# Seven block products instead of eight in part of an output projection, and weight loads of 1 MB

## The chip, the cores and the metric

One NeuronCore of a Trainium2 chip runs the whole kernel. The metric is the device time of one execution in microseconds (us). The engines are named as in the profile: PE (TensorE matmuls; PEld is its weight load), DVE (VectorE), ACT (ScalarE), POOL (GpSimd) and SP, whose queue issues the DMAs.

## The reference

One decoder layer on 256 tokens of width 4096, in fp32. Cut to what matters:

```python
proj = x @ w_in                        # 256 x 4096 by 4096 x 11280
y_conv, y_gla, y_mem = ...             # three gated groups; mem @ w_mem_kv feeds the third
mixed = concatenate([y_conv, y_gla, y_mem], axis=-1)      # 256 x 4096
out = mixed @ w_out                                       # 4096 x 4096
y = layernorm(alpha * x + out) * ln_g + ln_b
```

## The kernel before

An fp32 value is kept as two parts that the PE multiplies exactly: ACT casts it to `hi`, DVE subtracts to get `lo` (`halves`, L88 to L90). A product of two such values takes three passes: hi by hi, lo of the activations by hi of the weights, hi by lo of the weights. The activations are the stationary operand (128 features by 128 tokens), 512 columns of weights the moving one, and the sum over the 32 k-tiles of 128 features stays in one of eight PSUM banks.

The program has three parts. First the memory projection (L148 to L180): for each k-tile two weight loads of 512 KB, for four banks each; every fourth k-tile also one 512 KB unit of `memT` and one of `xT`. Then 23 panels of `w_in`, and after them 8 panels of `w_out` (the loop `for n in range(8)` near the end). `panel` takes 16 chunks of two k-tiles: a 512 KB load into one of six `raw` buffers (`wraw`), `halves` into one of four `hi` and four `lo` buffers (`whi`, `wlo`, WBUFS = 4), 24 matmuls over two token tiles into two of the four `acc` banks. So a `lo` can be made only when PE is through with the `lo` four tiles earlier, and a load can start only when the tile six earlier has been split. The next panel has the other two banks; after a panel DVE adds its banks to the residual rows (`residual`, L929) and takes statistics, and POOL multiplies by the norm's gain.

Small work (transposes, norms, gates) stands in a list and is dealt out between the chunks by `do_work`. The temporaries `T` and `S` (4 KB a partition each) exist once. The order of the instructions on each engine and of the DMAs on SP is fixed when the program is built, by a scheduler that sees the dependences and its own estimates; each engine then works strictly in that order. All loads go through SP's one queue.

Of the kernel before, what the change touches and what calls it, by code (L numbers as in the profile page):

```python
# [25 lines left out]
WBUFS = 4  # L26
# [6 lines left out]
# (name, index, column ranges of w_in)  # L33
# [15 lines left out]
def layer_kernel(ctx, tc, xT, memT, xres, w_mem, w_in, w_out, cst, w_gate,  # L49
# [5 lines left out]
    wraw = ctx.enter_context(tc.tile_pool(name="wraw", bufs=6))  # L55
# [7 lines left out]
    # SBUF in units of 4 KB a partition, each handed out again once it is given back  # L63
# [78 lines left out]
    # the array's clock comes up while the first loads are under way  # L142
# [3 lines left out]
    for kt in range(KT):  # L146
        if kt == 0:
            mt0 = unit_tiles("mem")  # L148
            m_units.append(load(mt0, four(memT[0]), 0, 1))
        elif kt % 4 == 0:  # L150
            m_units.append(load(unit_tiles("mem"), four(memT[kt // 4])))
        mh, ml = m_units[kt // 4]
        for half in range(2):
            wt = w_tiles([P, 1024], "wm")
            step = 256 if kt == 0 and half == 0 else 512
            if kt == 0:
                for a in range(0, 1024, step):
# [79 lines left out]
    def queue_halves(src, then):  # L237
        """Token-major [P, 2, 512] -> feature-major hi and lo, for then(hi, lo)."""

        def scratch():  # L240
            serial[0] += 1
            return tmp.tile([P, 4, 256], F32, tag="S", name=f"S_{serial[0]}", bufs=1)

        def go(d):
# [298 lines left out]
    def queue_head(h):  # L543
# [273 lines left out]
    # y = (z g) rstd - mu rstd g + b: z g as z comes, the rest a product of -mu rstd and 1  # L817
    # with g and b, g hi in rows 0 and 32, lo in 64, b hi in row 1, lo in 65
# [115 lines left out]
    for n in range(8):  # L934
        if 2 <= n < 6:
            work.append(lambda n=n: rows_gb(n - 2))
# [3 lines left out]
        if n < 7:  # L940
            banks = panel(w_out[n], 512, stat, soon=KT // 2 if n else 10)
            g = spread(ln_g, n, "S")
            for tt in range(2):
                residual(tt, n, banks[tt])
                y = z[n][:, tt, :]
                nc.gpsimd.tensor_tensor(out=y, in0=y, in1=g, op=ALU.mult)

    # the last panel ends with the first token tile, so that its norm runs beside the second's
    banks, rest = panel(w_out[7], 512, stat, apart=APART)
# [38 lines left out]
def lay_out(inputs):  # L988
# [67 lines left out]
```

## Time and profile before

| | |
|---|---|
| three runs | 1541.33, 1542.21, 1542.31 us (median 1542.21) |
| profiled execution | span 1539.6 us, from its first to its last instruction; a run's time has some 2.6 us more around such a span |
| PE busy | 1526.9 us (99%) |
| DVE, ACT busy | 980.6 us (64%), 740.7 us (48%) |
| DMA | 307.56 MB, mean 200 GB/s |

PE busy is the share of time in which some matmul is under way; since matmuls overlap, the pace is read from the time that a stretch of them takes, not from the duration of one.

### The profile page before, as it was taken

The page shows a single profiled execution, that of the slowest core. Times are in us where ns is not written, and L with a number is a line of the kernel's source. Part 1 is how long each engine was busy: PE and PEld are TensorE (multiplying, and loading weights), DVE is VectorE, ACT ScalarE, POOL GpSimd, SP SyncE. Part 2 cuts the span into 40 slices and gives each one's busy share as a digit, 9 for nine tenths or more (in the row PEclk, how much of TensorE's full clock was granted, in tenths as well). Part 3 has the DMA queues.
Part 4 walks back from the last instruction along what each step waited for, and adds up shares of the span by engine and source line. Part 5 has one row for each costly group of instructions (what it writes and reads, how often), then busy time and mean ns, then how long its engine had stood idle before and what let it go on. Part 6 is the DMA issues. An engine that isn't in the chain of part 4 may idle for free.

```text
span 1539.6 us, 18667 instructions
## 1 busy us (share of the span) xinstructions
PE 1526.9 (99%) x6977; PEld 1292.9 (84%) x6977; DVE 980.6 (64%) x1227; ACT 740.7 (48%) x898; POOL 68.0 (4%) x71
## 2 busy tenths in 40 slices
PE   9999999999999999999999999999999999999997
PEld 7888888888888888999998888888888888888885
DVE  6555654999999555857575555555557555455555
ACT  6444653444566344655454554455556333333341
POOL 0000000000000000003030000000000000000001
PEclk9999999999999999999999999999999999999998
DMA  8777676666656666565555566666677666666662
GB/s 326 245 251 249 190 210 193 190 197 188 193 163 178 218 192 188 161 191 175 167 170 195 179 195 205 193 193 195 195 233 253 216 196 196 206 202 199 198 199 109
DMA packets 89363, 307.56 MB, mean 200 GB/s; under 512 B 9972, under 2 KB 10868, under 8 KB 89272
## 3 DMA queue, kind: packets, MB, share of 16 engines
q1 hardware_dynamic: 89272, 306.38, 63.0%
q8 instruction: 54, 0.88, 0.2%
q14 instruction: 37, 0.30, 0.1%
HBM read 302.14 MB, written 4.19 MB: 199 GB/s over the span
## 4 chain that ended last, share of the span: by engine, by line
PE 98%; DVE 1%; DMA 0%; issue 0%; SPq 0%; ACT 0%; POOL 0%; DVEq 0%; ACTq 0%
PE acc L279 85%; PE mk L169 5%; PE mv L169 5%; PE o L260 1%; PE A L561 1%; PE sc L260 0%; PE mo L260 0%; DMA rawwm<-w_mem 0%; DVE xr L915 0%; SPq L115 0%; PE mg L905 0%; DVE nz L502 0%; POOL xr L913 0%; DVE cc L870 0%; DVE low L90 0%
## 5 line engine op out<-in xcount | busy, mean ns | idle before, releaser
L90 DVE TENSOR_TENSOR low<-raww,hiw 128x1024 fp32r<-128x1024 f32 (+2 forms) x496 | 603.5, 1219 | 427.5 <-ACT hiw L89 422.3
L89 ACT CAST hiw<-raww 128x1024 fp32r<-128x1024 f32 (+2 forms) x496 | 507.6, 1027 | 640.7 <-PE acc L279 612.4
L279 PE MATMUL acc<-hiw,hx 128*128 128x512 f32 (+2 forms) x1472 | 560.3, 381 | 0.0
L279 PE MATMUL acc<-hiw,lx 128*128 128x512 f32 (+2 forms) x1472 | 560.3, 381 | 0.0
L279 PE MATMUL acc<-low,hx 128*128 128x512 f32 (+2 forms) x1472 | 381.6, 380 | 0.0
L279 PEld LDWEIGHTS acc<-hiw,hx 128*128 128x128 f32 x1472 | 276.4, 188 | 45.4
L279 PEld LDWEIGHTS acc<-hiw,lx 128*128 128x128 f32 x1472 | 276.3, 188 | 45.2
L279 PEld LDWEIGHTS acc<-low,hx 128*128 128x128 f32 x1472 | 275.3, 188 | 45.4
L279 PE MATMUL acc<-hiw,xh 128*128 128x512 f32 x512 | 199.3, 389 | 0.0
L279 PE MATMUL acc<-hiw,xl 128*128 128x512 f32 x512 | 199.2, 389 | 0.0
L279 PE MATMUL acc<-low,xh 128*128 128x512 f32 x512 | 137.8, 389 | 0.0
L279 PEld LDWEIGHTS acc<-hiw,xl 128*128 128x128 f32 x512 | 96.1, 188 | 20.0
L279 PEld LDWEIGHTS acc<-low,xh 128*128 128x128 f32 x512 | 96.1, 188 | 19.9
L279 PEld LDWEIGHTS acc<-hiw,xh 128*128 128x128 f32 x512 | 96.1, 188 | 19.9
L90 DVE TENSOR_TENSOR lowm<-rawwm,hiwm 128x1024 fp32r<-128x1024 f32 (+2 forms) x68 | 78.3, 1160 | 53.2 <-ACT hiwm L89 52.6
L649 DVE SCALAR_TENSOR_TENSOR cacc<-hT,cst_sb,cacc 128x231 f32<-128x231 f32 (+29 forms) x240 | 98.0, 462 | 0.1
L89 ACT CAST hiwm<-rawwm 128x1024 fp32r<-128x1024 f32 (+2 forms) x68 | 67.6, 1002 | 62.8 <-PE mv L169 30.9
L169 PE MATMUL mk<-hiwm,hmem 128*128 128x512 f32 (+1 forms) x132 | 50.7, 387 | 0.4 <-ACT hiwm L89 0.4
L169 PE MATMUL mk<-hiwm,lmem 128*128 128x512 f32 (+1 forms) x132 | 50.4, 384 | 0.0
L227 ACT COPY S<-T 32x256 f32<-32x256 f32 x112 | 45.2, 404 | 9.9 <-DVE T L212 8.5
L169 PE MATMUL mv<-hiwm,hmem 128*128 128x512 f32 x128 | 49.9, 390 | 0.0
L169 PE MATMUL mv<-hiwm,lmem 128*128 128x512 f32 x128 | 49.8, 389 | 0.0
(179 smaller groups left out, 752.5 us busy)
## 6 DMA issues: line engine op xcount, KB each, us to landing
raww<-w_in SPq DMA_DIRECT2D x288, 512.0 KB
raww<-w_out SPq DMA_DIRECT2D x128, 512.0 KB
rawwm<-w_mem SPq DMA_DIRECT2D x62, 512.0 KB
raww<-w_in SPq DMA_DIRECT2D x64, 412.0 KB
raww<-w_in SPq DMA_DIRECT2D x16, 416.0 KB
rawx<-xT SPq DMA_DIRECT2D x8, 512.0 KB
xr<-xres SPq DMA_DIRECT2D x8, 512.0 KB
out<-xr SPq DMA_DIRECT2D x16, 256.0 KB
```

Source lines behind the costliest of these rows:

```text
L89: nc.scalar.copy(out=hi, in_=src)
L90: nc.vector.tensor_tensor(out=lo, in0=src, in1=hi.bitcast(F32), op=ALU.subtract)
L169: nc.tensor.matmul(mem_banks[half * 4 + a // 512 * 2 + mt][:, a % 512 : a % 512 + step], lhsT=s[:, kt % 4, mt * P : (mt + 1) * P], rhs=w[: ...
L227: f(out=to[32 * b : 32 * b + 32, :, :, a, :], in_=frm[32 * a : 32 * a + 32, :, :, b, :],)
L260: nc.tensor.matmul(ps, lhsT=a, rhs=b, start=t == 0 and k == 0, stop=t == n - 1 and k == 2)
L279: nc.tensor.matmul(banks[tt][:, :width], lhsT=s[:, kt % 4, tt * P : (tt + 1) * P], rhs=w[:, k, :], start=kt == 0 and not second and s is s ...
L561: nc.tensor.matmul(ps[:, at : at + n], lhsT=keys[:, j, k0 : k0 + P], rhs=qs[:, j, q0 : q0 + n], start=dk == 0, stop=dk == 1,)
L649: nc.vector.scalar_tensor_tensor(out=a, in0=h, scalar=dw_sb[:, cb, j : j + 1], in1=a, op0=ALU.mult, op1=ALU.add)
```

## The change

Output panels 0 to 5 are taken in three pairs. A pair's chunk is 1 MB: two k-tiles by two panels, four blocks of weights, against two k-tiles by two token tiles of activations. A chunk taken "by eight" is two tiles of 12 matmuls (`b`, `a`). A chunk taken "by seven" (Winograd's form of Strassen's product) needs seven block products, 21 matmuls: tile `c` (3), then `a`, `y`, `x` (6 each). DVE makes `x` and `y` as differences of weight blocks first, in the single temporaries `T` (`tx`) and `S` (`ty`), and all four are split. The sums of activation blocks are made once for a unit (`sums`, also through `S` and `T`) and kept. By seven go 4 of the 16 chunks of the first pair and 6 of each other. A pair uses all eight banks, N, 4, 3, 2 of `acc` and 1, 5, 6, 7 of `sm`; at its end DVE combines them into the residual rows, by way of `U`, which is `T` again, and multiplies by the gain. Besides, all weights come in 1 MB loads into three `raw` buffers of 8 KB, and the units of `memT` and `xT` are loaded into buffers of the general pool instead of `raw` buffers. Panels 6 and 7 keep their form.

```diff
-    wraw = ctx.enter_context(tc.tile_pool(name="wraw", bufs=6))
+    wraw = ctx.enter_context(tc.tile_pool(name="wraw", bufs=3))
...
-            wraw.tile([P, 4, 256], F32, tag="raw", name=f"raw{name}_{serial[0]}"),
+            unit([P, 4, 256], F32, f"raw{name}"),
...
+    def load_unit(name, ap):
+        tiles = unit_tiles(name)
+        hi, lo = load(tiles, ap)
+        give(tiles[0])
+        return hi, lo
...
-            m_units.append(load(unit_tiles("mem"), four(memT[kt // 4])))
+            m_units.append(load_unit("mem", four(memT[kt // 4])))
+        raw = w_raw([P, 2, 1024], "wm")
+        if kt:
+            nc.sync.dma_start(out=raw, in_=w_mem[kt].rearrange("p (h n) -> p h n", h=2))
...
-            x_units.append(load(unit_tiles("x"), four(xT[kt // 4])))
+            x_units.append(load_unit("x", four(xT[kt // 4])))
...
-            tiles = w_tiles([P, 2, width], "w", KT // 2 - apart <= c < KT // 2 - WBUFS)
-            hi, lo = load(tiles, chunks[c].rearrange("p (k n) -> p k n", k=2))
+            if c % 2 == 0:
+                raw = w_raw([P, 4, width], "w")
+                nc.sync.dma_start(out=raw, in_=chunks[c // 2].rearrange("p (k n) -> p k n", k=4))
+            hi, lo = w_tiles([P, 2, width], "w", KT // 2 - apart <= c < KT // 2 - WBUFS)
+            halves(raw[:, 2 * (c % 2) : 2 * (c % 2) + 2, :], hi, lo)
...
+    def sums(hi, lo):
+        r = tmp.tile([P, 4, 256], F32, tag="S", name=f"r_{serial[0]}", bufs=1)
+        f = tmp.tile([P, 2, 4, P], F32, tag="T", name=f"f_{serial[0]}", bufs=1)
+        nc.vector.tensor_tensor(out=r, in0=hi.bitcast(F32), in1=lo.bitcast(F32), op=ALU.add)
+        r = r.rearrange("p (q k) (t c) -> p q k t c", q=2, t=2)
+        a11, a21, a12, a22 = (r[:, :, k, t, :] for k in range(2) for t in range(2))
+        s1, s2, s3, s4 = (f[:, :, j, :] for j in range(4))
+        for o, x, y, op in (
+            (s1, a21, a22, ALU.add),
+            (s2, s1, a11, ALU.subtract),
+            (s3, a21, a11, ALU.subtract),
+            (s4, a12, s2, ALU.subtract),
+        ):
+            nc.vector.tensor_tensor(out=o, in0=x, in1=y, op=op)
+        eh = unit([P, 2, 4, P], F32R, "eh")
+        el = unit([P, 2, 4, P], F32R, "el")
+        halves(f, eh, el)
+        return eh, el
+    def pair(chunks, order, stat, ext, soon=KT // 2):
+        banks = {}
+        for pool, tag, names in ((acc, "acc", "N432"), (sm, "sm", "1567")):
+            for nm in names:
+                banks[nm] = pool.tile([P, 512], F32, tag=tag, name=f"{tag}_{nm}_{serial[0]}")
+        def plain(k, tt):
+            return lambda c: tuple(
+                t[:, (2 * c + k) % 4, tt * P : (tt + 1) * P] for t in stat(c // 2)
+            )
+        def summed(j):
+            return lambda c: tuple(t[:, c % 2, j - 1, :] for t in ext(c // 2))
+        a11, a21, a12, a22 = (plain(k, tt) for k in range(2) for tt in range(2))
+        eight = (
+            ("b", ((1, a21, "N"), (0, a22, "N"), (1, a11, "3"), (0, a12, "3"))),
+            ("a", ((0, a21, "4"), (1, a22, "4"), (0, a11, "2"), (1, a12, "2"))),
+        )
+        seven = (
+            ("c", ((0, summed(4), "3"),)),
+            ("a", ((1, a12, "2"), (0, a11, "1"))),
+            ("y", ((1, a22, "4"), (0, summed(2), "6"))),
+            ("x", ((0, summed(1), "5"), (1, summed(3), "7"))),
+        )
...
+        for n, (c, by7, tiles) in enumerate(plan):
+            raw = w_raw([P, 4, 512], "w")
+            nc.sync.dma_start(out=raw, in_=chunks[c].rearrange("p (k n) -> p k n", k=4))
+            w = {}
+            if by7:
+                x = tmp.tile([P, 2, 512], F32, tag="T", name=f"tx_{serial[0]}", bufs=1)
+                y = tmp.tile([P, 2, 512], F32, tag="S", name=f"ty_{serial[0]}", bufs=1)
+                nc.vector.tensor_tensor(
+                    out=x,
+                    in0=raw[:, 3:4, :].to_broadcast([P, 2, 512]),
+                    in1=raw[:, 0:3:2, :],
+                    op=ALU.subtract,
+                )
+                nc.vector.tensor_tensor(
+                    out=y[:, 0, :], in0=raw[:, 2, :], in1=x[:, 0, :], op=ALU.subtract
+                )
+                nc.vector.tensor_tensor(
+                    out=y[:, 1, :], in0=raw[:, 1, :], in1=y[:, 0, :], op=ALU.subtract
+                )
+                src = dict(a=raw[:, 0:2, :], c=raw[:, 2:3, :], x=x, y=y)
+            else:
+                src = dict(a=raw[:, 0:2, :], b=raw[:, 2:4, :])
+            for nm, terms in tiles:
+                m = 1 if nm == "c" else 2
+                w[nm] = tuple(t[:, :m, :] for t in w_tiles([P, 2, 512], "w"))
+                halves(src[nm], *w[nm])
+                for second in range(2):
+                    for j, (slot, st, bk) in enumerate(terms):
+                        sh, sl = st(c)
+                        for s in (sh,) if second else (sh, sl):
+                            nc.tensor.matmul(
+                                banks[bk],
+                                lhsT=s,
+                                rhs=w[nm][second][:, slot, :],
+                                start=first[bk] == (n, nm, j) and not second and s is sh,
+                                stop=last[bk] == (n, nm, j) and second == 1,
+                            )
+            do_work(-(-len(work) // max(1, soon - n)))
+        return banks
...
-    for n in range(8):
-        if 2 <= n < 6:
-            work.append(lambda n=n: rows_gb(n - 2))
+    def load_res(n):
         xr = unit([P, 2, 512], F32, "xr")
         nc.sync.dma_start(out=xr, in_=xres[n].rearrange("p (t d) -> p t d", t=2))
         z.append(xr)
...
+    extT = {}
+    def make_sums(u):
+        extT[u] = sums(*stat(u))
+    def in_order(pattern, by7):
+        p7 = [c for c in range(KT // 2) if c // 2 in by7]
+        p8 = [c for c in range(KT // 2) if c // 2 not in by7]
+        return [(p7.pop(0), True) if ch == "7" else (p8.pop(0), False) for ch in pattern]
+    orders = (
+        in_order("8888888887878787", (4, 5)),
+        in_order("8878878878788787", (4, 5, 6)),
+        in_order("8878878878788787", (4, 5, 6)),
+    )
+    for u in (4, 5):
+        work.append(lambda u=u: make_sums(u))
+    for j in range(3):
+        if j == 1:
+            work.append(lambda: make_sums(6))
+        n0, n1 = 2 * j, 2 * j + 1
+        load_res(n0)
+        load_res(n1)
+        b = pair(w_pairs[j], orders[j], stat, lambda u: extT[u], soon=KT // 2 if j else 8)
+        rows = [spread(ln_g, n0, "Ah"), spread(ln_g, n1, "Al")]
+        def add(y, ps, first=False):
+            if first:
+                nc.vector.scalar_tensor_tensor(
+                    out=y, in0=y, scalar=ALPHA, in1=ps, op0=ALU.mult, op1=ALU.add
+                )
+            else:
+                nc.vector.tensor_tensor(out=y, in0=y, in1=ps, op=ALU.add)
+        z11, z21 = z[n0][:, 0, :], z[n0][:, 1, :]
+        z12, z22 = z[n1][:, 0, :], z[n1][:, 1, :]
+        add(z22, b["N"], True)
+        add(z12, b["3"], True)
+        add(z11, b["2"], True)
+        add(z21, b["4"], True)
+        t = tmp.tile([P, 2, 512], F32, tag="T", name=f"U_{serial[0]}", bufs=1)
+        u2, u3 = t[:, 0, :], t[:, 1, :]
+        nc.scalar.copy(out=u2, in_=b["1"])
+        add(z11, b["1"])
+        nc.vector.tensor_tensor(out=u2, in0=u2, in1=b["6"], op=ALU.add)
+        add(z12, b["5"])
+        add(z22, b["5"])
+        nc.vector.tensor_tensor(out=u3, in0=u2, in1=b["7"], op=ALU.add)
+        add(z12, u2)
+        add(z21, u3)
+        add(z22, u3)
+        for n, tt, y in ((n0, 0, z11), (n1, 0, z12), (n0, 1, z21), (n1, 1, z22)):
+            nc.vector.bn_stats(out=stats[:, tt, n, :], in_=y)
+            nc.vector.tensor_tensor(out=y, in0=y, in1=rows[n - n0], op=ALU.mult)
...
```

The first place is SP's queue in the memory projection. Before, from the first load of k-tile 3 (`rawwm_241`) to k-tile 4 (`rawwm_303`, `rawwm_321`):

```order
L115 DMA rawwm_241<-w_mem 128x1024
L984 DMA ng_sb<-norm_g 128x512
L115 DMA rawwm_259<-w_mem 128x1024
L115 DMA rawx_291<-xT 128x1024
L115 DMA rawmem_297<-memT 128x1024
L115 DMA rawwm_303<-w_mem 128x1024
L115 DMA rawwm_321<-w_mem 128x1024
L115 DMA rawwm_339<-w_mem 128x1024
```

After the change, from the load of k-tile 3 (`rawwm_236`) to that of k-tile 4 (`rawwm_296`); 128x2048 is 1 MB, the others 512 KB:

```order
L162 DMA rawwm_236<-w_mem 128x2048
L116 DMA rawmem_290<-memT 128x1024
L116 DMA rawx_432<-xT 128x1024
L116 DMA rawmem_438<-memT 128x1024
L116 DMA rawx_580<-xT 128x1024
L116 DMA rawmem_586<-memT 128x1024
L116 DMA rawx_728<-xT 128x1024
L116 DMA rawmem_734<-memT 128x1024
L116 DMA rawx_876<-xT 128x1024
L116 DMA rawmem_882<-memT 128x1024
L162 DMA rawwm_296<-w_mem 128x2048
```

Two unit loads stood between the two k-tiles' weights, and now nine stand there.

The second place is DVE behind an output panel. Before, the last three splits of panel 1 with the first of panel 2, the two `residual` additions and the statistics:

```order
L90 TENSOR_TENSOR low_9950<-raww_9948,hiw_9949 128x1024
L90 TENSOR_TENSOR low_9978<-raww_9976,hiw_9977 128x1024
L90 TENSOR_TENSOR low_9996<-raww_9994,hiw_9995 128x1024
L929 SCALAR_TENSOR_TENSOR xr_9644<-xr_9644,acc_9646 128x512
L929 SCALAR_TENSOR_TENSOR xr_9644<-xr_9644,acc_9647 128x512
L90 TENSOR_TENSOR low_10014<-raww_10012,hiw_10013 128x1024
L932 BN_STATS zstats<-xr_9644 128x6 x2
L90 TENSOR_TENSOR low_10032<-raww_10030,hiw_10031 128x1024
```

After the change, behind the first pair: the end of the combination (`xr` are residual rows, `row` the gain), the sums for unit 6 (`r`, `f`, `eh` and `el`), and the second pair's first chunk by seven, whose `tx` has the place of `f`, which had the place of `U`:

```order
L1114 BN_STATS zstats<-xr_8891 128x6
L347 TENSOR_TENSOR f_9604<-r_9603 128x2x128 x2
L1115 TENSOR_TENSOR xr_8891<-xr_8891,row_9533 128x512
L1115 TENSOR_TENSOR xr_8889<-xr_8889,row_9531 128x512
L1115 TENSOR_TENSOR xr_8891<-xr_8891,row_9533 128x512
L347 TENSOR_TENSOR f_9604<-f_9604,r_9603 128x2x128
L347 TENSOR_TENSOR f_9604<-r_9603,f_9604 128x2x128
L90 TENSOR_TENSOR el_9611<-f_9604,eh_9610 128x1024
L398 TENSOR_TENSOR tx_9650<-raww_9648 128x1024
L404 TENSOR_TENSOR ty_9651<-raww_9648,tx_9650 128x512
L407 TENSOR_TENSOR ty_9651<-raww_9648,ty_9651 128x512
L90 TENSOR_TENSOR low_9673<-ty_9651,hiw_9672 128x1024
```

Where a split followed two additions, the `tx` of that chunk now stands behind the whole combination and the sums. Between the last split of the first pair (its tile `x`) and these rows DVE has 22 more instructions: 11 additions of the combination, `r`, six splits (four tiles of the second pair's two chunks by eight, tiles `c` and `a` of its first by seven), three statistics and one product with the gain. Behind the second pair it is the same list without `r`, `f` and `el`, with `tx` ahead of the last three products.

The third place is PE, in the second pair's first chunk by seven: the end of tile `a` (`hiw_9662`, `low_9663`) with what was put off, and the first matmuls of tile `y` (`hiw_9672`):

```order
L421 MATMUL sm_1005_9565<-hiw_9662,xh_8137 128x512
L421 MATMUL sm_1005_9565<-hiw_9662,xl_8138 128x512
L421 MATMUL acc_1002_9562<-low_9633,xh_6933 128x512 x2
L421 MATMUL acc_1004_9564<-low_9633,xh_6933 128x512 x2
L421 MATMUL acc_1004_9564<-hiw_9662,xh_8137 128x512
L421 MATMUL acc_1004_9564<-hiw_9662,xl_8138 128x512
L421 MATMUL acc_1003_9563<-low_9656,eh_8977 128x512
L421 MATMUL acc_1004_9564<-low_9663,xh_8137 128x512
L421 MATMUL sm_1005_9565<-low_9663,xh_8137 128x512
L421 MATMUL acc_1002_9562<-hiw_9672,xh_8137 128x512
L421 MATMUL acc_1002_9562<-hiw_9672,xl_8138 128x512
L421 MATMUL sm_1007_9567<-hiw_9672,eh_8977 128x512
```

Nothing stands between tiles `a` and `y`: where before any tile was a plain split of a load, PE's next matmul now needs `ty`.

## Rows read from the trace of the kernel before

**Rows 1.** The page: engines (busy us, share, instructions) and the chain by engine.
```profile
PE 1526.9 (99%) x6977; PEld 1292.9 (84%) x6977; DVE 980.6 (64%) x1227; ACT 740.7 (48%) x898; POOL 68.0 (4%) x71
...
PE 98%; DVE 1%; DMA 0%; issue 0%; SPq 0%; ACT 0%; POOL 0%; DVEq 0%; ACTq 0%
```

**Rows 2.** PE's waits over the whole span: total us, times, longest.
```profile
PE ccT L895 <- DVE cc L873: 4.3, 1, 4.3
PE mv L145 <- PEq L1038: 0.8, 1, 0.8
...
PE mk L169 <- ACT hiwm L89: 0.4, 1, 0.4
```

**Rows 3.** Stretches: busy us and instructions of each engine, granted clock, DMA share, GB/s.
```profile
0.00:40.00 40.00, 38.76 (x171) 30.48 (x172) 25.64 (x27) 24.00 (x28) 1.69 (x14) 1.00 0.88 323
1200.00:1240.00 40.00, 40.00 (x178) 33.12 (x177) 21.31 (x19) 15.56 (x15) 3.53 (x2) 1.00 0.63 201
```

**Rows 4.** The chain in order of time: start, duration, engine, line, matmuls.
```profile
133.59 2.72 PE mv L169 x12
...
842.96 675.93 PE acc L279 x2982
```

**Rows 5.** PE in order of time: the first matmuls, and the second k-tile's start.
```profile
0.84 3.14 PE L145 MATMUL mv<-const-bfloat16-1.0 128*128 128x512 bf16 x7 [0.84 <-PEq L1038]
...
9.40 1.09 PE L169 MATMUL mv<-lowm,hmem 128*128 128x512 f32 x4
10.90 0.51 PE L169 MATMUL mk<-hiwm,hmem 128*128 128x512 f32 x1 [0.40 <-ACT hiwm L89]
```

**Rows 6.** ACT in order of time, first loads: start, duration, idle before and releaser.
```profile
9.80 1.05 ACT L89 CAST hiwm<-rawwm 128x1024 fp32r<-128x1024 f32 x1 [1.18 <-DMA rawwm<-w_mem]
...
12.14 1.05 ACT L89 CAST hiwm<-rawwm 128x1024 fp32r<-128x1024 f32 x1 [0.78 <-DMA rawwm<-w_mem]
...
22.66 1.05 ACT L89 CAST hiwm<-rawwm 128x1024 fp32r<-128x1024 f32 x1 [0.29 <-DMA rawwm<-w_mem]
24.14 1.06 ACT L89 CAST hiwm<-rawwm 128x1024 fp32r<-128x1024 f32 x1 [0.43 <-DMA rawwm<-w_mem]
25.42 1.05 ACT L89 CAST hiwm<-rawwm 128x1024 fp32r<-128x1024 f32 x1 [0.22 <-DMA rawwm<-w_mem]
```

**Rows 7.** DVE's groups by line and shape: busy us, mean ns, idle before.
```profile
L90 DVE TENSOR_TENSOR low<-raww,hiw 128x1024 fp32r<-128x1024 f32 x416 | 515.8, 1242 | 382.6 <-ACT hiw L89 380.5 <-DMA raww<-w_in 1.5
L90 DVE TENSOR_TENSOR lowm<-rawwm,hiwm 128x1024 fp32r<-128x1024 f32 x62 | 75.3, 1223 | 51.1 <-ACT hiwm L89 50.6
...
L929 DVE SCALAR_TENSOR_TENSOR xr<-xr,acc 128x512 f32<-128x512 f32 x16 | 10.4, 684 | 13.5 <-PE acc L279 13.5
L932 DVE BATCH_NORM_STATS2 zstats<-xr 128x6 f32<-128x512 f32 x16 | 10.3, 682 | 0.1
...
L502 DVE TENSOR_TENSOR nz<-cs 128x1024 f32<-128x1024 f32 x2 | 2.8, 1411 | 0.0
...
L90 DVE TENSOR_TENSOR lowm<-rawwm,hiwm 128x256 fp32r<-128x256 f32 x4 | 1.6, 424 | 0.5 <-ACT hiwm L89 0.3
...
L90 DVE TENSOR_TENSOR lowm<-rawwm,hiwm 128x512 fp32r<-128x512 f32 x2 | 1.4, 692 | 1.7 <-ACT hiwm L89 1.7
...
L519 DVE TENSOR_TENSOR ca<-cs,el 128x256 f32<-128x256 f32 x2 | 1.2, 611 | 0.0
```

**Rows 8.** ACT's groups by shape in 1150:1540 us.
```profile
L89 ACT CAST hiw<-raww 128x1024 fp32r<-128x1024 f32 x134 | 141.1, 1055 | 203.9 <-PE acc L279 194.7 <-DVE low L90 6.7 <-DMA raww<-w_out 2.5
```

**Rows 9.** Stretches at the end of the program, columns as in Rows 3.
```profile
1526.00:1528.00 2.00, 0.00 (x0) 0.00 (x0) 1.49 (x6) 0.59 (x1) 2.00 (x3) 0.84 0.10 39
1528.00:1530.00 2.00, 0.48 (x1) 0.18 (x1) 1.97 (x3) 0.03 (x1) 1.13 (x1) 0.50 0.25 92
...
1533.00:1535.00 2.00, 1.03 (x2) 0.29 (x1) 2.00 (x4) 0.00 (x0) 0.00 (x0) 0.70 1.04 379
1535.00:1537.00 2.00, 0.00 (x0) 0.00 (x0) 0.82 (x2) 0.00 (x0) 0.00 (x0) 1.00 1.00 375
```

More of the change, by code (lines that the diff above doesn't have):

```diff
@@ L48, in layer_kernel @@
 @with_exitstack
-def layer_kernel(ctx, tc, xT, memT, xres, w_mem, w_in, w_out, cst, w_gate,
+def layer_kernel(ctx, tc, xT, memT, xres, w_mem, w_in, w_pairs, w_last, cst, w_gate,
                  conv_g, conv_b, norm_g, ln_g, ln_b, out):
@@ L90, in halves, with w_raw @@
         nc.vector.tensor_tensor(out=lo, in0=src, in1=hi.bitcast(F32), op=ALU.subtract)
+    def w_raw(shape, name):
+        serial[0] += 1
+        return wraw.tile(shape, F32, tag="raw", name=f"raw{name}_{serial[0]}")
     def w_tiles(shape, name, units=False):
@@ L94, in w_tiles @@
         s = serial[0]
-        raw = wraw.tile(shape, F32, tag="raw", name=f"raw{name}_{s}")
         if units:
-            return raw, unit(shape, F32R, f"hi{name}"), unit(shape, F32R, f"lo{name}")
+            return unit(shape, F32R, f"hi{name}"), unit(shape, F32R, f"lo{name}")
         return (
-            raw,
             whi.tile(shape, F32R, tag="hi", name=f"hi{name}_{s}"),
@@ L104, in unit_tiles @@
     def unit_tiles(name):
-        serial[0] += 1
         return (
-            wraw.tile([P, 4, 256], F32, tag="raw", name=f"raw{name}_{serial[0]}"),
+            unit([P, 4, 256], F32, f"raw{name}"),
             unit([P, 4, 256], F32R, f"h{name}"),
@@ L150, in layer_kernel @@
         elif kt % 4 == 0:
-            m_units.append(load(unit_tiles("mem"), four(memT[kt // 4])))
+            m_units.append(load_unit("mem", four(memT[kt // 4])))
         mh, ml = m_units[kt // 4]
+        raw = w_raw([P, 2, 1024], "wm")
+        if kt:
+            nc.sync.dma_start(out=raw, in_=w_mem[kt].rearrange("p (h n) -> p h n", h=2))
         for half in range(2):
-            wt = w_tiles([P, 1024], "wm")
+            wt = (raw[:, half, :], *w_tiles([P, 1024], "wm"))
             step = 256 if kt == 0 and half == 0 else 512
@@ L157, in layer_kernel @@
                 for a in range(0, 1024, step):
-                    hi, lo = load(wt, w_mem[kt, half], a, a + step)
+                    hi, lo = load(wt, w_mem[kt][:, 1024 * half : 1024 * half + 1024], a, a + step)
                 if half == 1:
@@ L161, in layer_kernel @@
             else:
-                hi, lo = load(wt, w_mem[kt, half])
+                hi, lo = wt[1:]
+                halves(*wt)
                 if kt == 1 and half == 0:
                     load(mt0, four(memT[0]), 2, 4)
+                    give(mt0[0])
             for w, stats in ((hi, (mh, ml)), (lo, (mh,))):
@@ L308, in panel @@
         return banks, rest
+    def sums(hi, lo):
+        serial[0] += 1
+        r = tmp.tile([P, 4, 256], F32, tag="S", name=f"r_{serial[0]}", bufs=1)
[15 more added lines that the diff above has]
+        return eh, el
@@ new lines, in pair @@
+    def pair(chunks, order, stat, ext, soon=KT // 2):
+        banks = {}
+        for pool, tag, names in ((acc, "acc", "N432"), (sm, "sm", "1567")):
+            for nm in names:
+                serial[0] += 1
+                banks[nm] = pool.tile([P, 512], F32, tag=tag, name=f"{tag}_{nm}_{serial[0]}")
[16 more added lines that the diff above has]
+        )
+        plan = [(c, by7, seven if by7 else eight) for c, by7 in order]
+        first, last = {}, {}
+        for n, (_, _, tiles) in enumerate(plan):
+            for nm, terms in tiles:
+                for j, (_, _, bk) in enumerate(terms):
+                    first.setdefault(bk, (n, nm, j))
+                    last[bk] = (n, nm, j)
+        for n, (c, by7, tiles) in enumerate(plan):
[3 more added lines that the diff above has]
+            if by7:
+                serial[0] += 1
+                x = tmp.tile([P, 2, 512], F32, tag="T", name=f"tx_{serial[0]}", bufs=1)
[15 more added lines that the diff above has]
+                src = dict(a=raw[:, 0:2, :], b=raw[:, 2:4, :])
+            for nm, terms in tiles:
+                m = 1 if nm == "c" else 2
[14 more added lines that the diff above has]
+        return banks
@@ L717, in layer_kernel @@
         size = 16 * P * 2 * width
-        chunks = w_in[off : off + size].rearrange("(c p f) -> c p f", c=16, p=P)
+        chunks = w_in[off : off + size].rearrange("(c p f) -> c p f", c=8, p=P)
         off += size
@@ L939, in layer_kernel @@
         z.append(xr)
[L940 to L949, printed above, removed]
+    extT = {}
[5 more added lines that the diff above has]
+        return [(p7.pop(0), True) if ch == "7" else (p8.pop(0), False) for ch in pattern]
@@ new lines, in layer_kernel @@
+    orders = (
[26 more added lines that the diff above has]
+        add(z21, b["4"], True)
+        serial[0] += 1
+        t = tmp.tile([P, 2, 512], F32, tag="T", name=f"U_{serial[0]}", bufs=1)
[12 more added lines that the diff above has]
+            nc.vector.tensor_tensor(out=y, in0=y, in1=rows[n - n0], op=ALU.mult)
@@ L950, in layer_kernel @@
+    for e in extT.values():
+        give(*e)
+    for j in range(4):
+        work.append(lambda j=j: rows_gb(j))
+    load_res(6)
+    load_res(7)
+    banks = panel(w_last[0], 512, stat)
+    g = spread(ln_g, 6, "S")
+    for tt in range(2):
+        residual(tt, 6, banks[tt])
+        y = z[6][:, tt, :]
+        nc.gpsimd.tensor_tensor(out=y, in0=y, in1=g, op=ALU.mult)
+    banks, rest = panel(w_last[1], 512, stat, apart=APART)
     g, beta = spread(ln_g, 7, "S"), spread(ln_b, 7, "Ah")
@@ L999, in chunks, with pair_chunks @@
         n = w.shape[1]
-        return w.reshape(16, 2, P, n).transpose(0, 2, 1, 3).reshape(16, P, 2 * n)
+        return w.reshape(8, 4, P, n).transpose(0, 2, 1, 3).reshape(8, P, 4 * n)
+    def pair_chunks(w, a):
+        b = w[:, a : a + 1024].reshape(16, 2, P, 2, 512)
+        blocks = [b[:, k, :, j, :] for k, j in ((0, 0), (1, 0), (1, 1), (0, 1))]
+        return np.stack(blocks, axis=2).reshape(16, P, 2048)
     x, w_in, w_out = g["x"][0], g["w_in"][0], g["w_out"][0]
@@ L1020, in lay_out @@
         "xres": x.reshape(2, P, 8, 512).transpose(2, 1, 0, 3).reshape(8, P, 1024),
-        "w_mem": g["w_mem_kv"][0].reshape(KT, P, 2, 1024).transpose(0, 2, 1, 3),
+        "w_mem": g["w_mem_kv"][0].reshape(KT, P, 2048),
         "w_in": np.concatenate(panels),
-        "w_out": np.stack([chunks(rows[:, 512 * i : 512 * i + 512]) for i in range(8)]),
+        "w_pairs": np.stack([pair_chunks(rows, 1024 * j) for j in range(3)]),
+        "w_last": np.stack([chunks(rows[:, 512 * i : 512 * i + 512]) for i in (6, 7)]),
         "cst": cst,
```

## Prediction

> **What bounds the kernel now.** I read the page first: PE is busy 99% of the span, and the chain that ended last is 98% PE [rows 1]. Then PE's waits: the longest is 4.3 us in the last norm, and only 0.4 us lies ahead of a weight tile, at the start [rows 2]. Then the chain in order of time for PE's pace: 12 matmuls take 2.72 us in the memory projection, and 2982 take 675.93 us in one unbroken piece from 843 us through most of the output projection [rows 4]. That is 226.7 ns for one matmul of 512 columns. Last the stretches: in the output projection DVE works 21.3 us of 40 and DMA 63%, with the clock at 1.00 (the 2.4 GHz level), but in the first 40 us DMA is at 88% and 323 GB/s [rows 3]. So PE is the bound from end to end, matmuls taken away count in full, and every new gap in PE counts in full as well.
>
> **What goes.** 4 + 6 + 6 = 16 chunks by seven save 3 matmuls each: 48 x 0.2267 = 10.9 us.
>
> **1 MB loads at the start.** ACT's casts show when loads land, since each waits for its DMA: 12.14, 22.66, 24.14, 25.42 us [rows 6]. Between the first and the last of these landed k-tile 2 (1 MB), the constants (0.38 MB), k-tile 3 (1), one unit of x and one of mem (1), k-tile 4 (1) and half of 5 (0.5): 4.88 MB in 13.28 us, 2.72 us per MB. The queue is thus never empty here; a single 512 KB took 1.28 to 1.48 us, which bounds the rate at 2.56 to 2.96.
>
> K-tile 1 now waits for 1 MB where it waited for 512 KB. Half of it landed at 9.80 [rows 6]; the whole lands at 9.80 + 0.5 x 2.72 = 11.16. The cast takes 1.05 us and PE began 0.05 us behind it, at 10.90 [rows 5]; now at 12.26, 1.4 us late.
>
> K-tile 4 stands behind nine unit loads (order of SP). From k-tile 1 to its landing pass 0.25 (mem) + 1 (k-tile 2) + 0.38 + 0.5 (x) + 1 (k-tile 3) + 4.5 (the nine) + 1 = 8.63 MB: 23.5 us, so it lands at 34.6 and PE can begin at 35.7. PE is through with k-tiles 1 to 3 at 12.26 + 3 x 5.44 = 28.6. It stands for 7.1 us; with the two rates 5.7 to 9.2. The loads that are early this way help nobody, since later PE never waited for one.
>
> The page DMA: Bandwidth & Descriptors of the Trainium skill says (Queues, rings and completion order) that each DMA engine takes the descriptors of a ring in order, though completions need not come in order. By that rule the nine loads are paid ahead of k-tile 4. The trace agrees: the unit loads and weights landed in the order of issue. The same page (Bandwidth, Measured) asks for transfers of at least 1 MB and gives 425 GB/s for 16 MB; at that rate, as an estimate, the 8.63 MB would take 21.3 us and the gap 4.9. No row here shows such a rate over a long stretch.
>
> **The clock behind a gap.** At the end PE stands from 1525 to 1529 us: the granted clock is 0.84 in 1526 to 1528, so it fell to 0.50 (the 1.2 GHz level) at about 1527.4; it is 0.70 in 1533 to 1535, so back at about 1534.2, 4.7 us after PE began again, and 1.00 then [rows 9]. The first seven matmuls run at 0.45 us each too [rows 5]. A gap that long so costs up to 4.7/2 = 2.35 us more; I take 2.1, between 0 and 2.35.
>
> **The pairs on DVE.** Prices: 1024 columns 1.22 us, 512 columns 0.69, PSUM addition 0.68 (I count 0.69), statistics 0.68, 256 columns 0.42 [rows 7]; ACT's cast 1.05 [rows 8]. Of operands with a repeated part the trace shows 1.41 for 1024 and 0.61 for 256 [rows 7]; `tx` and `f` could cost that, 0.2 and 0.8 us more in all. `tx` reads long runs, so I take the plain price.
> A chunk by seven needs on DVE `tx` 1.22, two `ty` 1.38, `c` 0.69, three splits 3.66: 6.95 us for 21 matmuls (4.76 us); one by eight 2.44 for 5.44. Alternating, DVE has 9.4 us to do in PE's 10.2. That holds, barely. A pair's end adds 11 to 12 additions, four statistics, four products: 13 us, on a DVE with no room.
>
> Let 0 be PE's first matmul of the second pair. DVE's split of the first pair's last tile `x` must wait for PE's `lo` four tiles earlier, 16 matmuls before 0 (-3.6); with the wait for the cast of `y` it ends at about -2.0 (at best -2.4, at worst 0). From there to the second `ty` of the next chunk by seven stand 34 instructions: 8 of 1024 columns (9.8), 18 of 512 (12.4), 4 statistics (2.7), 4 `f` (1.7), in all 26.6, and 1.05 in which `el` waits for ACT's `eh`. So `ty` is done at 25.7, its cast at 26.7. PE has until then two chunks by eight (48 matmuls), 2 put off of `x`, and `c` and `a` (9): 59 x 0.2267 = 13.4 us. Gap: 13.3 us (12.9 to 16). No other order is open: `tx` needs the place of `f`, `f` that of `U`, and `U` the banks.
>
> Behind the second pair `r`, `f`, `el` are missing: 6 of 1024 columns (7.3), 18 of 512 (12.4), 4 statistics (2.7) = 22.5; `ty` at 20.5, cast at 21.5, gap 8.1 us (7.7 to 10.5). Behind the third comes panel 6, which needs no `tx`; its second bank is that of product 4, added at 2.5 where PE asks at 1.4: 1.2 us (0 to 2). POOL loses the products and waits for nobody. The first pair starts with idle `sm` banks and chunks by eight: nothing.
>
> **Sum** against the profiled execution (span 1539.6): -10.9 + 1.4 + 7.1 + 13.3 + 8.1 + 1.2 + 3 x 2.1 = +26.5, span 1566.1. Its own time with the 2.6 us around the span agrees with the median of the runs, 1542.2; so 1568.7 us. By the bounds: -10.9 + 1.2 + 5.7 + 12.9 + 7.7 + 0 + 0 = +16.6, to -10.9 + 1.6 + 9.2 + 16 + 10.5 + 2 + 7 = +35.4: 1559 to 1578.
>
> **Rivals.** (1) *Loads overtake*: k-tile 4 gets its share of the DMA engines at once and PE doesn't stand at 28 us. For it: 16 engines, and 88% busy leaves room. Against: landings in the order of issue. It would take 7.1 + 2.1 off and half of the 1.4: 1558.8.
> (2) *Not slower: DVE's chain is covered.* Place: the two ends of pairs. Price: 13.3 + 8.1 and two clocks, 25.6. It decides if DVE is 13 us ahead there, that is if `ty` stands by the time PE is through with tile `a`. For it: DVE had 47% free. Against: four `lo` buffers let it be ahead by at most four tiles, which are 4.8 us in a chunk by seven. Then -10.9 + 10.6 + 1.2: 1543.1, no change in effect; with (1) besides, 1533.
> (3) *DVE bounds the pairs*: its instructions take 1.24 us as in the mean of 416 splits [rows 7] or more, `tx` 1.41, and the 0.8 us of room in each 10.2 is gone. From about 10% dearer, each of the 16 chunks by seven adds 0.5 to 1 us, and the time is about 1582.
> (4) *The seven products don't save*: matmuls on summed blocks or switching banks run slower. Before, PE changes bank with every token tile and keeps its pace; 10.9 us is the price, 1580.
>
> **Chances.** Forecast 0.67, (1) 0.13, (2) 0.11 of which 0.06 with (1), (3) and (4) 0.09. A difference under 0.2% (3 us) can't be told from none here. Faster 0.07, within 0.2% 0.04, slower 0.89. The range reaches down to (1) with its bounds and up to (3): 1550 to 1583; (2) is left out.
>
> **What would show it.** In the trace after: PE waits for ACT's cast of a weight tile at about 28 us for about 7 us, with ACT waiting for `rawwm`; twice behind a pair for ACT's cast of `ty`, 13 and 8 us, and DVE busy without a break there; the clock at 0.50 behind each; 48 matmuls fewer. I am wrong if PE's chain shows no gap over 3 us at these places, or if DVE stands idle in front of `tx`.

## The result and the profile after

The changed kernel takes 1562.69 us (median of 4 runs, 1562.20 to 1564.77) against 1542.12 us (1541.33 to 1542.31): slower by 20.6 us, ratio 1.0136, 95% interval [1.0122, 1.0151]. The forecast was 1568.7 us with a range of 1550 to 1583. The span of the profiled execution is 1561.1 us against 1539.6, 21.5 us more.

The page of the changed kernel, its first engine row and the shares of the chain of waits (the work that ended last, followed back through whatever released it), and then PE's waits (what PE waited for: us in total, times, longest):

```profile
PE 1523.4 (98%) x6929; PEld 1288.4 (83%) x6929; DVE 1069.3 (68%) x1361; ACT 769.7 (49%) x936; POOL 46.8 (3%) x59
...
PE 94%; DVE 3%; DMA 2%; issue 0%; ACT 0%; SPq 0%; POOL 0%; DVEq 0%; ACTq 0%
```

```profile
PE acc L421 <- ACT hiw L89: 16.2, 2, 10.8
PE mk L181 <- ACT hiwm L89: 9.3, 3, 7.6
PE ccT L1016 <- DVE cc L994: 4.3, 1, 4.3
```

Against [rows 1]: 48 matmuls fewer (6977 to 6929), and in a chain that was 98% PE the share of DVE has gone from 1 to 3% and that of DMA from 0 to 2%. Against [rows 2]: PE waited 0.4 us for a weight tile, and now 25.5 us, at the start and behind the first two pairs. The 4.3 us in the last norm are the same.

**The start.** The chain of waits of the changed kernel (start, us, what), where the chain before had one load of 5.21 us at 4.56 and from 10.90 us on only PE, and ACT's casts beside it (start, us of a piece, what, idle before and what ended it), where [rows 6] had weights between:

```profile
4.56 7.18 DMA rawwm<-w_mem
11.76 11.18 DMA rawx<-xT
23.00 12.87 DMA rawwm<-w_mem
37.07 3.78 PE mk L181 x8
```

```profile
25.75 1.05 ACT L89 CAST hmem<-rawmem 128x1024 fp32r<-128x1024 f32 x1 [1.36 <-DMA rawmem<-memT]
27.03 1.06 ACT L89 CAST hx<-rawx 128x1024 fp32r<-128x1024 f32 x1 [0.23 <-DMA rawx<-xT]
...
33.41 1.04 ACT L89 CAST hmem<-rawmem 128x1024 fp32r<-128x1024 f32 x1 [0.23 <-DMA rawmem<-memT]
35.97 1.99 ACT L89 CAST hiwm<-rawwm 128x1024 fp32r<-128x1024 f32 x2 [1.51 <-DMA rawwm<-w_mem]
```

One unit after the other lands every 1.28 us, and only behind them k-tile 4. PE stands meanwhile (PE's timeline, same columns):

```profile
12.86 0.50 PE L181 MATMUL mk<-hiwm,hmem 128*128 128x512 f32 x1 [1.58 <-ACT hiwm L89]
...
37.07 0.80 PE L181 MATMUL mk<-hiwm,hmem 128*128 128x512 f32 x1 [7.59 <-ACT hiwm L89]
37.66 0.63 PE L181 MATMUL mk<-hiwm,lmem 128*128 128x512 f32 x1
```

K-tile 1 begins at 12.86 instead of 10.90 [rows 5]. Behind the 7.59 us matmuls start 0.43 us apart instead of 0.23 until 40.65.

**The ends of pairs.** The chain of waits behind the first pair, from where it leaves PE on:

```profile
1273.55 0.60 DVE U L1106
1274.15 1.13 DVE low L90
...
1280.02 0.61 DVE zstats L1114
...
1286.00 1.81 DVE xr L1115 x3
1287.81 0.35 DVE f L347
...
1288.63 1.05 ACT eh L89
...
1289.71 1.24 DVE el L90
...
1290.97 1.24 DVE tx L398
...
1292.95 0.70 DVE ty L407
...
1293.73 1.05 ACT hiw L89
...
1294.83 1.22 PE acc L421 x2
```

This is the chain that the prediction wrote down: U, statistics and products, `f`, `eh`, `el`, `tx`, `ty`, ACT's cast, PE. PE ran out of work at 1284.02. Behind the second pair the same chain without `f`, `eh` and `el` ends in a gap of 5.4 us at 1386.14. Behind the third there is none: panel 6's two banks follow each other at PE's pace (chain of waits):

```profile
1457.47 0.91 PE acc L291 x4
1458.38 0.45 PE sm L421 x2
1458.83 16.32 PE acc L291 x72
```

**The clock** (stretches: us, busy us and instructions of each engine, granted clock, DMA share, GB/s), behind the start's gap and the first pair's:

```profile
36.00:40.00 4.00, 2.93 (x7) 2.35 (x8) 2.81 (x3) 3.49 (x4) 0.00 (x0) 0.50 1.00 408
40.00:44.00 4.00, 4.00 (x16) 3.23 (x16) 2.09 (x3) 2.66 (x4) 0.00 (x0) 0.88 1.05 419
...
1296.00:1298.00 2.00, 2.00 (x7) 1.52 (x6) 2.00 (x3) 2.00 (x3) 0.00 (x0) 0.50 0.87 369
...
1300.00:1302.00 2.00, 2.00 (x9) 1.56 (x9) 2.00 (x3) 0.12 (x1) 0.00 (x0) 0.88 0.63 209
```

0.50 is the 1.2 GHz level. Behind the first pair the first 14 matmuls take 5.9 us from start to start (1294.83 to 1300.75) and would take 3.2 at full pace: 2.7 us lost. At the start it is 1.9 (10 matmuls in 4.2 us), behind the second pair 1.6 (10 in 3.8); the forecast's 2.1 came from [rows 9].

Sum of what was measured: -10.9 (48 x 0.2267) + 2.0 (k-tile 2 begins at 18.43 instead of 16.47) + 7.6 + 10.8 + 5.4 + 6.2 (clock) + 0.5 = +21.6, against 21.5. The 0.5 is 3 x 0.16: each wait is counted from the end of a matmul that lasts 0.39 us, though the next would have started 0.23 us behind its start.

### The profile page after: what moved, and what is told of

It is laid out like the page before. It is cut to its first block, busy times and chain, and to the rows that moved or that the text cites. A ratio compares the mean times of both kernels' runs of the same rounds, so it can differ in the third digit from the quotient of the medians.

```text
span 1561.1 us, 18190 instructions
## 1 busy us (share of the span) xinstructions
PE 1523.4 (98%) x6929; PEld 1288.4 (83%) x6929; DVE 1069.3 (68%) x1361; ACT 769.7 (49%) x936; POOL 46.8 (3%) x59
## 4 chain that ended last, share of the span: by engine, by line
PE 94%; DVE 3%; DMA 2%; issue 0%; ACT 0%; SPq 0%; POOL 0%; DVEq 0%; ACTq 0%
PE acc L291 67%; PE acc L421 9%; PE mk L181 5%; PE mv L181 5%; PE sm L421 3%; PE acc_N L421 3%; DMA rawwm<-w_mem 1%; DMA rawx<-xT 1%; DVE low L90 1%; PE o L272 1%; PE A L682 1%; DVE xr L1093 0%; PE sc L272 0%; PE mo L272 0%; DVE xr L1115 0%
## 5 line engine op out<-in xcount | busy, mean ns | idle before, releaser
L90 DVE TENSOR_TENSOR low<-raww,hiw 128x1024 fp32r<-128x1024 f32 (+3 forms) x496 | 586.3, 1187 | 329.5 <-ACT hiw L89 316.2
L89 ACT CAST hiw<-raww 128x1024 fp32r<-128x1024 f32 (+3 forms) x496 | 499.4, 1012 | 556.3 <-PE acc L291 470.6
L421 PE MATMUL acc<-hiw,xh 128*128 128x512 f32 x224 | 88.0, 393 | 16.2 <-ACT hiw L89 16.2
L421 PE MATMUL acc<-hiw,xl 128*128 128x512 f32 x224 | 87.6, 391 | 0.0
L421 PE MATMUL acc<-low,xh 128*128 128x512 f32 x224 | 66.9, 390 | 0.0
L421 PEld LDWEIGHTS acc<-hiw,xh 128*128 128x128 f32 x224 | 42.2, 189 | 25.8 <-ACT hiw L89 17.1
L291 PE MATMUL acc<-hiw,xh 128*128 128x512 f32 x128 | 49.9, 390 | 0.0
L291 PE MATMUL acc<-hiw,xl 128*128 128x512 f32 x128 | 49.8, 389 | 0.0
```

The lines of the kernel that those rows point to most:

```text
L291: nc.tensor.matmul(banks[tt][:, :width], lhsT=s[:, kt % 4, tt * P : (tt + 1) * P], rhs=w[:, k, :], start=kt == 0 and not second and s is s ...
L421: nc.tensor.matmul(banks[bk], lhsT=s, rhs=w[nm][second][:, slot, :], start=first[bk] == (n, nm, j) and not second and s is sh, stop=last[b ...
```

## The experiments

Theory A is the order of loads on SP, theory B the amount of work that stands ahead of `ty` in DVE's order. Each run was timed beside the kernel before on the same chip (1541.8 to 1542.1 us).

**e1_units_in_ring**, theory A against the rate of DMA.

```diff
-            unit([P, 4, 256], F32, f"raw{name}"),
+            w_raw([P, 4, 256], name),
```

> The raw tiles of x and mem units take a place in the ring of three again, so their loads can't run ahead; weights still come as 1 MB loads. Theory A (order on SP): k-tile 4 no longer stands behind nine unit loads, the gap of 7.6 us at 29 us and the slow clock behind it (1.9 us) go; k-tile 1 stays 1.8 us late; the ends of pairs stay. 1562.7 - 7.6 - 1.9 = 1553.2 us. Rival (rate: 1 MB loads are too slow for PE at the start, in any order): PE still stands before k-tiles 2 to 5, and the time stays within 2 us of 1562.7.

Measured 1554.91 us (1554.71 to 1555.86), ratio 1.0086 [1.0069, 1.0103]. The gap before k-tile 4 is gone, and its cast begins at 28.95 us instead of 35.97, so the order of the loads made the gap and not their rate. The 1.7 us over the forecast fit a fall of the clock behind the short wait for k-tile 1, whose 24 matmuls take 7.2 us here and 5.6 in the changed kernel (PE's timeline, then the stretch; in the changed kernel this stretch has 1.00):

```profile
13.06 0.50 PE L179 MATMUL mk<-hiwm,hmem 128*128 128x512 f32 x1 [1.90 <-ACT hiwm L89]
```

```profile
14.00:16.00 2.00, 2.00 (x6) 1.59 (x5) 2.00 (x3) 0.48 (x1) 0.00 (x0) 0.50 0.45 188
```

**e2_own_places**, theory B against the shared place alone.

```diff
-                x = tmp.tile([P, 2, 512], F32, tag="T", name=f"tx_{serial[0]}", bufs=1)
+                x = unit([P, 2, 512], F32, "tx")
...
+            if by7:
+                give(x)
...
-        t = tmp.tile([P, 2, 512], F32, tag="T", name=f"U_{serial[0]}", bufs=1)
+        t = unit([P, 2, 512], F32, "U")
...
+        give(t)
```

> U and tx get places of their own instead of the one place that tx, f and U share; the work is the same. Theory B (the amount of work on DVE that stands, in its order, ahead of ty): the gap shrinks only by what the new order puts behind ty. Counted in the new order at 1.14 and 0.60 us from start to start, 22.5 us stand ahead of ty behind the first pair instead of 25.3, gap 8.0 instead of 10.8; 12.3 instead of 20.1 behind the second, gap 0 instead of 5.4 and no slow clock (1.7): 1562.7 - 2.8 - 5.4 - 1.7 = 1552.8 us. Rival C (the shared place alone): with a place of its own tx is made in time at both ends, both gaps and their clock go, 1562.7 - 10.8 - 2.9 - 5.4 - 1.7 = 1541.9 us.

Measured 1553.55 us (1551.39 to 1553.94), ratio 1.0072 [1.0057, 1.0087]. PE's waits in 1180 to 1310 us and in 1310 to 1400:

```profile
PE acc L421 <- ACT hiw L89: 7.3, 1, 7.3
...
PE acc L421 <- ACT hiw L89: 0.2, 1, 0.2
```

Theory B's 8.0 and 0 were near; rival C's "both gone" falls. A place of its own lets `tx` move ahead, but what counts is how many instructions are left ahead of `ty`.

**e3_products_on_pool**, less work on DVE.

```diff
-            nc.vector.tensor_tensor(out=y, in0=y, in1=rows[n - n0], op=ALU.mult)
+            nc.gpsimd.tensor_tensor(out=y, in0=y, in1=rows[n - n0], op=ALU.mult)
```

> The four products with the gain at a pair's end go back from DVE to POOL; places are as in the changed kernel. Theory B: 4 x 0.60 us less on DVE ahead of ty at each end, gaps 8.4 and 3.0 us: 1562.7 - 2.4 - 2.4 = 1557.9 us, or up to 2 less where a clock fall goes too. Rival C: the products hold no shared place, so nothing changes, 1562.7 us.

Measured 1562.93 us (1562.27 to 1565.20), ratio 1.0139 [1.0124, 1.0154]: rival C's number, but for another reason. The timelines of POOL and of DVE behind the first pair and, the last line, behind the second:

```profile
1279.28 7.37 POOL L1115 TENSOR_TENSOR xr<-xr,row 128x512 f32<-128x512 f32 x4 [90.38 <-DVE zstats L1114]
...
1281.39 1.87 DVE L1114 BATCH_NORM_STATS2 zstats<-xr 128x6 f32<-128x512 f32 x3
1283.17 2.35 DVE L347 TENSOR_TENSOR f<-r 128x256 f32<-128x256 f32 x2
1285.45 1.48 DVE L347 TENSOR_TENSOR f<-f,r 128x256 f32<-128x256 f32 x1
1286.96 0.42 DVE L347 TENSOR_TENSOR f<-r,f 128x256 f32<-128x256 f32 x1
...
1380.44 1.64 DVE L404 TENSOR_TENSOR ty<-raww,tx 128x512 f32<-128x512 f32 x1
```

Beside POOL's products an `f` takes 0.95 to 1.48 us, and 0.42 as soon as POOL is through (1286.65); a `ty` takes 1.64 instead of 0.69. The three statistics, with one operand in SBUF, keep their pace. It goes both ways: POOL's first product, which begins beside a split and two additions of DVE with both operands in SBUF, takes 3.35 us, and the shortest of the four 1.27, while that split and those additions keep their 1.20 and 0.68. What DVE no longer multiplies it so loses by waiting: the gaps are 11.1 and 5.6 us. The Trainium skill says (SBUF — State Buffer, SBUF: two separate sides) that a DVE instruction with two SBUF inputs and a GpSimd instruction that reads SBUF take one pair of ports for the whole of an instruction, and that the other blocks; these rows agree. The kernel before had it too: beside its two products (1264.53 to 1268.06 us) splits take 1.94 and 1.64 us instead of 1.22, but DVE had room there.

**e4_early_sums**, less work behind the first pair alone.

```diff
-    for u in (4, 5):
+    for u in (4, 5, 6):
         work.append(lambda u=u: make_sums(u))
...
-        if j == 1:
-            work.append(lambda: make_sums(6))
```

> The third make_sums (unit 6) is made ahead of the first pair with the other two, so r, f, the wait for eh and el leave the first pair's end. Theory B: 20.0 us stand ahead of ty instead of 25.3, so the first gap becomes like the second, 5.4 us with 1.7 of slow clock; the second stays: 1562.7 - 5.4 - 1.2 = 1556.1 us. Rival C: tx still needs the place of U, which comes free with the last addition of U; DVE does that at 1282.9, so ty would stand at 1286 and the gap would be about 3 us: 1562.7 - 7.8 - 2.9 = 1552 us.

Measured 1558.47 us (1557.78 to 1560.78), ratio 1.0110 [1.0095, 1.0125]. The gaps are 5.6 and 5.4 us, as theory B had them; C's 3 us for the first falls. The time is 2.4 over the forecast. The profiled execution, the slowest of the four, shows where it has 3.1 us more than the changed kernel: not at the pairs but in the middle of the input projection (first line; the changed kernel's is the second):

```profile
722.00:724.00 2.00, 2.00 (x10) 1.99 (x10) 1.57 (x2) 0.46 (x1) 0.00 (x0) 0.50 0.56 158
```

```profile
722.00:724.00 2.00, 2.00 (x13) 2.00 (x13) 1.84 (x3) 0.96 (x2) 0.08 (x1) 1.00 0.46 102
```

PE waits 0.63 and 0.75 us there in this run, 0.65 and 0.75 in the changed kernel's. The clock fell in one and not in the other.

**e5_places_early** joins e2 and e4.

> Places of their own for U and tx, and the third make_sums ahead of the first pair; the products stay on DVE, the start as in the changed kernel. Theory B (work on DVE in its order ahead of ty): counted in the new order, 13.5 us stand ahead of ty behind the first pair (5 of 1024 columns at 1.14, 12 of 512 and one statistics at 0.60); PE comes to ty's tile 14.5 us behind the same point, so there is no gap behind the first pair and none behind the second: 1562.7 - 20.8 = 1541.9 us. Rival D (DVE has too much to do over a pair, whatever its order): the gap comes back at a later chunk by seven, each pair's end costs at least 3 us, 1548 us or more.

Measured 1544.31 us (10 runs, 1542.45 to 1545.24), ratio 1.0013 [1.0003, 1.0022]; the profiled execution is the 1542.45. Gaps of 0.6 and 0.3 us and no slow clock behind the pairs: D falls, DVE has time enough over a pair. The median's other 1.9 us lie in executions without a trace and stay open.

**e7_all_by_eight** takes the seven products away; 1 MB loads and the start stay.

```diff
-        in_order("8888888887878787", (4, 5)),
-        in_order("8878878878788787", (4, 5, 6)),
-        in_order("8878878878788787", (4, 5, 6)),
+        in_order("8" * 16, ()),
+        in_order("8" * 16, ()),
+        in_order("8" * 16, ()),
...
-        add(z11, b["1"])
```

> All chunks of the three pairs by eight products: no sums of blocks, no tx and ty, four additions at a pair's end; 1 MB loads and the start as in the changed kernel. Theory: seven products save PE 10.9 us, and their sums and additions cost 20.8 us in gaps and slow clock, so without them 48 matmuls come back and the gaps go: 1562.7 + 10.9 - 20.8 = 1552.8 us, with the gap of 6 to 8 us at the start and none behind pairs. Rival (products on sums of blocks run slower on PE and save nothing): 1541.9 us or less.

Measured 1552.37 us (1551.61 to 1554.20), ratio 1.0067 [1.0053, 1.0080]. It begins the long piece of the input projection at 190.68 us, as e5 does; its span is 1550.4 against 1540.7 with e5's 0.9 us of gaps: seven products save 10.6 us of PE. So the changed kernel gains that, and loses more at the ends of its pairs.

**e8_all_mended** joins e1 and e5 and loads k-tile 1 in two halves.

> Everything together: raw tiles of units in the ring again, k-tile 1 loaded in two halves of 512 KB, own places for U and tx, the third make_sums early. Theory: nothing is left of the four delays but up to 2 us at the start, and the 48 matmuls are saved: 1541.8 - 10.9 + 0 to 2 = 1531 to 1533 us, faster than both kernels. Rival D (DVE too busy over a pair): 1537 us or more, with gaps of 3 us or more behind the pairs.

Measured 1535.91 us (1534.10 to 1538.59), ratio 0.9961 [0.9948, 0.9973]: faster than both, but 3 us over the upper end of the forecast. The pairs are through with 1.6 us of waits. At the start PE stands again before k-tile 4 (PE's timeline):

```profile
31.81 0.80 PE L181 MATMUL mk<-hiwm,hmem 128*128 128x512 f32 x1 [2.69 <-ACT hiwm L89]
```

In the chain of waits its load (4.90 us) begins at 25.71, where DVE's split of an earlier weight tile ends. Units now take places of weight tiles in a ring of three; that this holds the load up is the reading that e9 tests.

**e9_units_in_two_places** gives the units two small places outside the ring.

```diff
-            unit([P, 4, 256], F32, f"raw{name}"),
+            tmp.tile([P, 4, 256], F32, tag="S" if name == "mem" else "T", name=f"raw{name}_{serial[0]}", bufs=1),
```

> As the run with everything together, but the raw tiles of x and mem units have one place of 512 KB each outside the weights' ring, so a unit's load waits for its forerunner's split and takes no weight tile's place. Theory A: k-tile 4 stands behind one unit load only, and no weight tile waits for a unit's place; the 2.7 us before k-tile 4 and the slow clock behind it (1.5 us) go, k-tile 1 stays about 1.2 us late: 1535.9 - 4.2 = 1531.7 us, at most 1533. Rival (1 MB loads in a ring of three are too coarse for the start): PE still stands 2 us or more before some k-tile, 1535 us or more.

Measured 1533.26 us (1532.38 to 1535.59), ratio 0.9946 [0.9934, 0.9959]: 8.7 us under the kernel before. PE's waits, and the stretch behind the one of 2.4 us, for k-tile 1:

```profile
PE ccT L1018 <- DVE cc L996: 4.3, 1, 4.3
PE mk L181 <- ACT hiwm L89: 2.7, 2, 2.4
...
PE acc L421 <- ACT hiw L89: 0.9, 2, 0.6
```

```profile
14.00:16.00 2.00, 2.00 (x6) 1.61 (x5) 1.94 (x3) 1.08 (x2) 0.00 (x0) 0.50 1.03 393
```

K-tile 4 comes in time. K-tile 1 is late by 2.4 us although it is loaded in halves; its first half is cast at 12.23, where [rows 6] had 9.80. Its load is issued at 4.55 us, as before (4.56), and takes 7.65 us instead of 5.21. Why stays open.

**e10_early_pool** is e5 with the products on POOL.

> Own places for U and tx and the third make_sums early, start as in the changed kernel, and the four products of a pair's end on POOL. Theory P (a POOL product and a DVE instruction with two operands in SBUF hold each other up): splits, tx and ty beside the four products (7 us of POOL) take 1.6 us or more instead of 0.7 to 1.2; the 1.0 us that DVE is ahead there is gone, 3 to 5 us more than with the products on DVE: 1547 to 1551 us, with gaps behind the pairs. Rival (POOL's work is free for DVE): DVE has 2.4 us less at each end, no gap, 1544.3 us or up to 1 less.

Measured 1544.36 us (1543.59 to 1546.78), ratio 1.0018 [1.0009, 1.0027], as e5. Theory P's 3 to 5 us don't come: splits beside POOL are longer, two of them 3.94 us instead of 2.35, but behind `ty`, where DVE has room, and the gaps stay at 0.3 and 1.0 us. That POOL holds DVE up stands by the rows; that it costs time does only where DVE's order is on the path.

## Why the prediction was right, point by point

- **Slower, and by what**: right. All three gaps are where they were forecast, with the releasers that were named. The forecast change of the span, 26.5 us, is 5.0 too much. The time, 1568.7, is 6.0 too much: the 2.6 us around a span set a median against the span of one execution; in every execution on record that lists both, it is 1.7 to 1.8.
- **Matmuls saved, -10.9**: right; 48 fewer, and 10.6 us between e5 and e7. Rival (4) falls.
- **K-tile 1, +1.4**: 2.0, and the reason given, waiting for 1 MB instead of 512 KB, isn't borne out: e8 and e9 load it in halves, and PE still begins it 1.25 and 2.4 us late. In the changed kernel, e1, e8 and e9 DMA moves 165 to 212 GB/s in 6 to 8 us, and 321 before; the cause stays open.
- **K-tile 4, 7.1 (5.7 to 9.2)**: 7.6 here, and 4.5 to 6.5 in the other six runs with this start, so the closeness is in part luck. DMA moved 411 GB/s in 20 to 28 us and 422 in 28 to 36, about the rate for which the prediction's other estimate had 4.9 us; the gap was 7.6 even so. e1 and e9 show the order on SP as the cause; rival (1) falls.
- **Clock, 3 x 2.1**: 1.9, 2.7 and 1.6. The sum is right, by luck: two were priced too high and one too low. That one costs at most 2.35 is wrong.
- **Pairs, 13.3 and 8.1**: 10.8 and 5.4. This is the step that was mis-sized. The count of instructions was right and so was PE's deadline: in the chain of waits its first matmul of the second pair is at 1270.65, and 13.37 us later it stops, 59 x 0.2267. The price was not: the prediction added mean durations, 1.22 and 0.69 us [rows 7], but DVE begins the next instruction before that time is over, if nothing holds it. DVE's timeline of the changed kernel:

```profile
1277.53 0.68 DVE L1093 TENSOR_TENSOR xr<-xr,sm 128x512 f32<-128x512 f32 x1
1278.13 0.68 DVE L90 TENSOR_TENSOR low<-raww,hiw 128x512 fp32r<-128x512 f32 x1
1278.73 0.68 DVE L1109 TENSOR_TENSOR U<-U,sm 128x512 f32<-128x512 f32 x1
```

  Each lasts 0.68 and the next starts after 0.60. Over 34 instructions 0.08 us each are 2.7 us, against a miss of 2.5 at the first end; over 28 they are 2.2, of 2.7 at the second. The trace of before had it too, where splits stand close:

```profile
1186.60 1.22 DVE L90 TENSOR_TENSOR xl<-S,xh 128x1024 fp32r<-128x1024 f32 x1
1187.73 2.35 DVE L90 TENSOR_TENSOR low<-raww,hiw 128x1024 fp32r<-128x1024 f32 x2
```

  The Trainium skill says so (Perfetto Trace Analysis, DVE / Act Engine Instruction): a shown duration ends with the acknowledged write, and the next instruction may begin to read before that. With 1.14 and 0.60, e2, e4 and e5 were forecast to within 0.7 us at each gap. Only where an instruction needs its forerunner's result (`tx` to `ty`) does the whole duration count.
- **"No other order is open"**: right for the changed kernel; with places of their own `tx` and U move, and that alone is worth 3.5 us at the first end and 5.2 at the second (e2).
- **Panel 6, 1.2**: 0, because the reading of the banks was wrong, not because DVE was faster. Product 4 is added last, and PE begins panel 6's second bank before that addition ends (timelines of DVE and PE):

```profile
1458.34 0.68 DVE L1089 SCALAR_TENSOR_TENSOR xr<-xr,acc 128x512 f32<-128x512 f32 x1
```

```profile
1458.67 0.39 PE L291 MATMUL acc<-hiw,xh 128*128 128x512 f32 x1
```

  In the program that bank is the one of product 3, which DVE added at 1454.87.
- **Rivals (2) and (3)**: (2) needed DVE 13 us ahead, and it was not; but e5 shows that with less ahead of `ty` the pairs do run through. (3) falls: `tx` takes 1.22 us, no more for its repeated part.

## What to carry to other kernels

Work that is saved on the bound engine is worth what the others can follow; at a seam (a change of panel, a first use of a new buffer) count the instructions in order ahead of the one that is waited for, and price a row of independent ones by their distance from start to start. A pool that limited how far loads run ahead did a second job: when tiles move to a larger pool, look what then stands ahead in the queue. Moving work to POOL frees DVE only where DVE's instructions beside it don't take two operands from SBUF, or where DVE isn't waited for.

## What the runs showed of the hardware

Waits of PE of one length don't always cost the same clock. At k-tile 1 the clock kept 1.00 behind 1.58 us (the changed kernel) and 2.12 (e5), and fell to 0.50 behind 1.87 (e10), 1.90 (e1) and 2.38 (e9). Such a fall costs 1.6 to 3.1 us, as much as some edits here, so it can make single executions of one kernel differ; e4's 1557.78 to 1560.78 may be an example, but only its slowest execution has a trace.
